# A decoder trunk of three token mixers: early weights in quarters, value products one accumulator at a time, an indexer that stays in PSUM, and last rows that end on three engines

## The chip, the cores and the metric

The kernel runs on one core of one Trainium2 chip. TensorE (PE) multiplies matrices, VectorE (DVE), ScalarE (ACT) and GpSimd (POOL) work on elements, and SyncE (SP) issues DMA transfers. The metric is the time of one execution in microseconds on the device.

## The reference

The input x has 512 rows of 1024 numbers. One projection feeds three mixers side by side: A, a pooling mixer with trailing windows of 2, 4, 8 and 16; B, sparse attention, in which an indexer scores the keys for each query and the 128 best are kept; C, attention in three branches (compressed blocks, selected blocks, a window), added with gates. Each is gated, projected to 1024 columns and merged; one output projection and a LayerNorm follow. What the change touches:

```python
rel = jax.nn.relu(jnp.einsum('bthd,bsd->bths', iqb, ik))          # B: the indexer
score = jnp.einsum('bths,bth->bts', rel, iwb).astype(jnp.float32)
...
_, idx = lax.top_k(score, topk)
...
p = _masked_softmax(s, valid).astype(v.dtype)
return jnp.einsum('bthk,btkd->bthd', p, vg)                       # B: the value product
...
p_c = _masked_softmax(s_c, m_c)                                   # C: compressed blocks
o_c = jnp.einsum('btgrn,bngd->btgrd', p_c.astype(vcmp.dtype), vcmp)
...
outs.append(mean - xg[:, :, g].astype(jnp.float32))               # A: window mean less x
...
return ((xf - mu) * lax.rsqrt(var + LN_EPS) * g + b).astype(x.dtype)
```

## The kernel before

**Products.** Every projection is computed in three matmuls for each piece of 128 inputs (L68 to L70): the operands are split into a high and a low part, and high x high, low x high and high x low are added in PSUM. The high part of a weight tile is made by ScalarE (L93 or L64), the low part by a subtraction on GpSimd (L95, in most of the program) or VectorE (L65). A tile of 128 output columns for all 512 rows takes 8 x 3 matmuls of 512 columns.

**Order.** TensorE executes in program order, and that order is written out by hand in `manual_schedule`. A stream of filler work F (projections, gates, merges) is stepped a few products at a time between the parts of the attention "units". The other engines' orders are chosen by the compiler's scheduler.

**Head.** Eight idle matmuls (L103) run while the first data arrives. The tiles of w0 and w3 come in halves, in turn with the eight pieces of x (L129), and the keys' projection takes two steps with w0, then two with w3.

**Indexer.** For row tiles 1 to 3 and eight heads a matmul writes 128 rows of scores in one of four PSUM slots ("qps"), ScalarE applies ReLU into a tile `rel` in SBUF (L292), and VectorE adds rel times a weight to `acc` (L294, L296). Sixteen rounds of MAX8 and MATCH_REPLACE (L305, L306) then find the best keys of each row tile.

**Attention units.** A unit is a row tile j of a branch: "c" units of branch C (g = 0, 1; two branches each), "b" units of branch B (b00 to b13: group, row tile). Its front computes query-key products in the same four slots (L442), mask and row extreme (L444), exponential (L449, ScalarE), the scale r (L453 to L457), and two f16 parts of the probabilities (pb or pc, L461 and L463), which a DMA transposes (L470). Its back, at least two sub-units later, is the value product (L480) into one of two halves of one PSUM bank (`ACC`), and `finish` (L535, VectorE) scales and gates it into yb or yc. `flush` takes units in pairs: both products stand next to each other in TensorE's order.

**Compressed blocks.** `Compressed.probs` subtracts the row extreme (L512, VectorE) and takes one exponential of four heads at once (L513). `compress_v` spreads the compressed values over a block-diagonal tile VC by multiplying with a 0/1 mask (L397, six VectorE instructions).

**End.** For each of four row tiles the output projection is followed by mean and variance and two passes, (z - mean) x gain (L925) and x scale + bias (L927). In tiles 0 to 2 VectorE does 768 columns and GpSimd 256; in the last tile VectorE does all 1024 in two pieces, each stored from SP's queue (L928).

Of the kernel before, what the change touches and what calls it, by code (L numbers as in the profile page):

```python
# [7 lines left out]
F32 = mybir.dt.float32  # L8
# [20 lines left out]
SMALL = (("posk", 32), ("posv", 32), ("pool_b", 4), ("pool_scale", 4), ("bmask", 4), ("rcnt", 16), ("rowv", 1),  # L29
# [5 lines left out]
def trunk(ctx, tc, a, out, dbg=None):  # L35
# [66 lines left out]
    for _ in range(8):  # L102
        nc.tensor.matmul(ps, idle[:, :128], idle, start=True, stop=True)  # L103
# [24 lines left out]
    with tc.high_priority():  # L128
        for k in "a01b23c4d567":  # L129
            if k in "abcd":  # L130
                load_early(EARLY["abcd".index(k) % 2], "abcd".index(k) // 2, 2)
            else:
                dma = load_x(int(k))
# [151 lines left out]
    def index_scores(j):  # L285
        n = (j + 1) * 128
        acc = cp.tile([128, n], F32, name=f"acc{j}")
        for h in range(8):
            ps = qps(f"is{j}{h}")[:, :n]
            nc.tensor.matmul(ps, QI[h][:, (j - 1) * 128:j * 128], KI[:, :n], start=True, stop=True)  # L290
            rel = big("b", "rel", F32, (128, 512))[:, :n]
            nc.scalar.activation(rel, ps, AF.Relu)  # L292
            if h == 0:
                nc.vector.tensor_scalar(acc, rel, IW[:, j, 0:1], None, op0=OP.mult)  # L294
            else:
                nc.vector.scalar_tensor_tensor(acc, rel, IW[:, j, h:h + 1], acc, op0=OP.mult, op1=OP.add)  # L296
            yield
        dg = acc[:, j * 128:n]
        nc.vector.tensor_add(dg, dg, cmask[:, 384:512])
        dbg(f"score{j}", acc)  # L300
        negm[j] = acc
# [13 lines left out]
    VC = [cp.tile([128, 2, 4, 64], BF, name=f"vc{p}") for p in range(3)]  # L315

# [65 lines left out]
    def compress_v():  # L382
        HH, HL, w2h, w2l = CP["v"] + W2[1]
        bmask = small["bmask"]
        v32 = sp.tile([128, 2, 64], F32, name="vc32", bufs=1)
        ps = dps("vc")[:, :128].rearrange("p (g d) -> p g d", g=2)
        for g in range(2):
            mm3(ps[:, g], HH[:, g].rearrange("p r n -> p (r n)"), HL[:, g].rearrange("p r n -> p (r n)"),
                w2h, w2l, True, True)
        nc.vector.tensor_scalar(v32, ps, vscale, 0.5, op0=OP.mult, op1=OP.mult)  # L390
        for p in range(3):
            v1 = sp.tile([128, 2, 64], BF, name="vc1", bufs=2)
            nc.vector.tensor_copy(v1, v32)
            if p < 2:
                nc.vector.tensor_sub(v32, v32, v1)
            for g in range(2):
                nc.vector.tensor_mul(VC[p][:, g], v1[:, g, None, :].to_broadcast([128, 4, 64]),  # L397
                                     bmask[:, :, None].to_broadcast([128, 4, 64]))
        yield
# [85 lines left out]
    class Compressed:  # L485
# [5 lines left out]
        def begin(self, j, Q, K):  # L491
# [4 lines left out]
            if j == NT - 1:  # L496
                ps = dps("sc")[:, :128].rearrange("p (h n) -> p h n", h=4)
                for h in range(4):
                    q = Q[h // 2][:, h % 2, j * 128:(j + 1) * 128]
                    for z in range(2):  # L500
                        nc.tensor.matmul(ps[:, h], q, K[:, z, :32], start=z == 0, stop=z == 1)
                nc.vector.tensor_add(self.s, ps, mcmp[:, j, None].to_broadcast([128, 4, 32]))
                nc.vector.tensor_reduce(self.mx[:, :4], self.s, AX.X, OP.max)

# [4 lines left out]
        def probs(self):  # L509
            g, j, s = self.g, self.j, self.s  # L510
            den, r = sm("cden", 4, 2), sm("cr", 4, 2)
            nc.vector.tensor_sub(s, s, self.mx[:, :4, None].to_broadcast([128, 4, 32]))  # L512
            nc.scalar.activation(s, s, AF.Exp, scale=self.scale)  # L513
# [43 lines left out]
    def pool_x(g):  # L557
# [14 lines left out]
        nc.vector.tensor_sub(e[:, :w - 1], e[:, :w - 1], x0[:, :w - 1])  # L572
        nc.vector.scalar_tensor_tensor(x0, cur, 1.0 / w, x0, op0=OP.mult, op1=OP.subtract)
        nc.vector.tensor_copy(x0[:, :w - 1], e[:, :w - 1])
# [157 lines left out]
    for n in (2, 1, 1, 1, 1, 1, 2):  # L732
# [48 lines left out]
    def flush(limit):  # L781

        while backs and (limit == 1000 or len(backs) > 1 and backs[1][0] <= limit):
            pair, n = backs[:2], 0
            del backs[:2]
            if limit == 1000:
                F.step(12)
            for _, un, (kind, g, j, br) in pair:
# [4 lines left out]
            for _, un, (kind, g, j, br) in pair:  # L793
# [13 lines left out]
    for w in work:  # L807
# [28 lines left out]
        backs.append((nsub, un, w))  # L836
# [63 lines left out]
    for t in range(NT):  # L900
# [15 lines left out]
        cut = (0, 512, 1024) if last else (0, 384, 768, 1024)  # L916
        cs = [slice(c0, c1) for c0, c1 in zip(cut, cut[1:])]
        if not last:
            c = cs.pop()
            nc.gpsimd.tensor_scalar(z[:, c], z[:, c], mv[:, 0:1], y, op0=OP.subtract, op1=OP.mult)  # L920
            nc.gpsimd.tensor_mul(z[:, c], z[:, c], lng[:, c])
            nc.gpsimd.tensor_add(z[:, c], z[:, c], lnb[:, c])
# [3 lines left out]
        for c in cs:  # L926
            nc.vector.scalar_tensor_tensor(z[:, c], z[:, c], y, lnb[:, c], op0=OP.mult, op1=OP.add)  # L927
            nc.sync.dma_start(out[t * 128:(t + 1) * 128, c], z[:, c])  # L928


def layout(v):
# [50 lines left out]
    r["bmask"] = (t[:, None] // 32 == np.arange(4)[None]).astype(f4)  # L982
# [19 lines left out]
```

## Time and profile before

| | |
|---|---|
| Median of 3 runs | 537.79 us (534.98 to 538.72) |
| The profiled execution | 536.65 us, of which the span of the profile is 534.9 |
| TensorE busy | 510.4 us (95%), 2718 matmuls |
| VectorE busy | 380.2 us (71%) |
| ScalarE busy | 278.4 us (52%) |
| GpSimd busy | 218.5 us (41%) |
| DMA | 66.72 MB, mean 125 GB/s |

The span is cut by stage as follows: until about 52 us the first projections, to about 92 the indexer beside other projections, to about 300 the units of branch C with the top-k rounds and the filler, to about 410 the units of branch B, then merges and the output projection, from 525.75 the last rows without TensorE. A matmul of 512 columns shows 0.39 us when TensorE has its full clock and 0.63 at the half; one starts 0.23 or 0.43 after the other. In a row of a timeline the bracket at the end is the idle time ahead of the instruction and what ended it.

### The profile page before, as it was taken

How to read it: one execution, taken by the hardware profiler on the slowest of the kernel's cores; microseconds unless marked ns; L12 is line 12 of the kernel's file. 1: busy time of each engine (PE TensorE's matmuls, PEld its weight loads, DVE VectorE, ACT ScalarE, POOL GpSimd, SP SyncE). 2: the span in 40 equal slices, each digit the busy share in tenths (PEclk: the TensorE clock that was granted, in tenths of full speed). 3: DMA queues.
4: the chain of work that ended last, by engine and by line, in shares of the span. 5: the costliest groups of instructions: out<-in, count | busy, mean ns of one | idle time of the engine just before them, and what ended most of it. 6: DMA issues, size and time to landing. Idle time of an engine off the chain costs nothing. (4 is left out here: it accounts for less than half of the span.)

```text
span 534.9 us, 7764 instructions
## 1 busy us (share of the span) xinstructions
PE 510.4 (95%) x2718; PEld 423.7 (79%) x2718; DVE 380.2 (71%) x928; ACT 278.4 (52%) x561; POOL 218.5 (41%) x190
## 2 busy tenths in 40 slices
PE   8999999999999998999998995999899999999993
PEld 5899878888888886788887884887787888887883
DVE  5774798898769898997898879565653345554276
ACT  6783465667655666565546564575553245342000
POOL 0425433436553756153534534227651212116043
PEclk9999989999999999999999998899999999999997
DMA  8622331363854434364545636256444435463012
GB/s 286 256 79 80 112 126 60 87 148 86 183 139 123 119 85 117 63 181 124 140 121 104 132 110 145 49 138 138 119 119 134 141 137 187 148 205 110 1 69 89
DMA packets 82135, 66.72 MB, mean 125 GB/s; under 512 B 67184, under 2 KB 68656, under 8 KB 82096
## 3 DMA queue, kind: packets, MB, share of 16 engines
q1 hardware_dynamic: 74912, 40.54, 28.5%
q0 software_dynamic: 7184, 25.69, 16.1%
q8 instruction: 21, 0.34, 0.3%
q14 instruction: 18, 0.15, 0.1%
HBM read 47.87 MB, written 2.10 MB: 93 GB/s over the span
## 5 line engine op out<-in xcount | busy, mean ns | idle before, releaser
L68 PE MATMUL d<-xh,w_h 128*128 128x512 f32 (+1 forms) x424 | 167.5, 395 | 2.6 <-ACT z L153 2.2
L69 PE MATMUL d<-xl,w_h 128*128 128x512 f32 (+1 forms) x424 | 165.8, 391 | 0.0
L70 PE MATMUL d<-xh,w_l 128*128 128x512 f32 (+1 forms) x424 | 165.5, 390 | 0.0
L95 POOL TENSOR_TENSOR w_l<-w_st,w_h 128x1024 fp32r<-128x1024 f32 x41 | 99.5, 2428 | 127.1 <-ACT w_h L93 120.4
L68 PEld LDWEIGHTS d<-xh,w_h 128*128 128x128 f32 x424 | 80.5, 190 | 18.3 <-ACT z L153 2.6
L70 PEld LDWEIGHTS d<-xh,w_l 128*128 128x128 f32 x424 | 80.3, 189 | 16.9
L69 PEld LDWEIGHTS d<-xl,w_h 128*128 128x128 f32 x424 | 80.4, 190 | 14.1
L93 ACT ACTIVATE w_h<-w_st 128x1024 fp32r<-128x1024 f32 x53 | 56.2, 1060 | 36.9 <-DMA w_st<-in_wt_dram 20.5
L449 ACT ACTIVATE qkc<-qkc,nb 128x512 f32<-128x512 f32 (+3 forms) x64 | 32.0, 501 | 49.8 <-DVE nb L444 32.0
L95 POOL TENSOR_TENSOR wp_l<-wp_st,wp_h 128x512 fp32r<-128x512 f32 x16 | 20.8, 1297 | 48.3 <-ACT wp_h L93 48.3
L641 POOL TENSOR_TENSOR m<-m,tg 128x512 f32<-128x512 f32 x12 | 17.5, 1457 | 54.2 <-DVE tg L615 54.0
L463 DVE SCALAR_TENSOR_TENSOR pc<-qkc,r,pc 128x512 f16<-128x512 f32 (+3 forms) x64 | 32.4, 544 | 8.2 <-ACT pc L461 7.9
L461 ACT ACTIVATE pc<-qkc,r 128x512 f16<-128x512 f32 (+3 forms) x64 | 29.5, 525 | 15.1 <-DVE r L457 7.2
L444 DVE CUSTOM_DVE_ANT_0 qkc<-qkc,cmask 128x512 f32<-128x512 f32 (+3 forms) x64 | 31.2, 493 | 2.9 <-PE qkc L442 2.5
L449 ACT ACTIVATE qkb<-qkb,nb 128x128 f32<-128x128 f32 (+3 forms) x32 | 16.0, 499 | 23.1 <-DVE nb L444 22.8
L92 POOL DMA_DIRECT2D w_st<-in_wt_dram x41 | 23.3, 569 | 9.9 <-POOL w_l L95 5.9
L70 PE MATMUL wo<-woh,ml 128*128 128x512 f32 (+1 forms) x72 | 26.4, 367 | 0.6 <-DVE ml L65 0.6
L69 PE MATMUL wo<-wol,mh 128*128 128x512 f32 (+1 forms) x72 | 26.3, 366 | 0.0
L68 PE MATMUL wo<-woh,mh 128*128 128x512 f32 (+1 forms) x72 | 26.3, 365 | 0.0
L306 DVE MATCH_REPLACE8 acc<-m,acc 128x256 f32<-128x256 f32 (+2 forms) x48 | 25.9, 541 | 0.0
L305 DVE MAX8 m<-acc 128x8 f32<-128x256 f32 (+2 forms) x48 | 25.2, 548 | 0.1
L68 PE MATMUL pp<-yh,wp_h 128*128 128x512 f32 x64 | 25.1, 392 | 0.0
(249 smaller groups left out, 1015.3 us busy)
## 6 DMA issues: line engine op xcount, KB each, us to landing
w_st<-in_wt_dram POOLq DMA_DIRECT2D x41, 512.0 KB, 3.7
w_st<-in_wt_dram SPq DMA_DIRECT2D x12, 512.0 KB, 4.4
wp_st<-in_wp_dram POOLq DMA_DIRECT2D x16, 256.0 KB, 3.0
wo_st<-in_wo_dram SPq DMA_DIRECT2D x8, 512.0 KB, 3.5
xst<-in_xT_dram SPq DMA_DIRECT2D x8, 256.0 KB, 4.8
wp_st<-in_wp_dram SPq DMA_DIRECT2D x8, 256.0 KB, 2.6
z<-in_x_dram SPq DMA_DIRECT2D x4, 512.0 KB, 5.1
wvst<-in_wve_dram SPq DMA_DIRECT2D x4, 320.0 KB, 7.1
```

The costliest lines, as they stand in the source:

```text
L68: nc.tensor.matmul(ps, wh, rh, start=start, stop=False)
L69: nc.tensor.matmul(ps, wh, rl, start=False, stop=False)
L70: nc.tensor.matmul(ps, wl, rh, start=False, stop=stop)
L92: (nc.gpsimd if POOL[0] else nc.sync).dma_start(st, src)
L93: nc.scalar.activation(h[:, :n], st, AF.Copy)
L95: eng.tensor_sub(l[:, :n], st, f(h[:, :n]))
L305: nc.vector.max(m8, negm[j])
L306: nc.vector.match_replace(negm[j], m8, negm[j], MARK)
L444: nc.vector.tensor_tensor_reduce(sc[i], sc[i], self.mask, -0.125, 3e38, OP.add, OP.min, nb[:, i:i + 1])
L449: nc.scalar.activation(sc[i], sc[i], AF.Exp, scale=-1.0, bias=nb[:, i:i + 1], accum_out=den[:, i:i + 1])
L461: nc.scalar.activation(p[:, 0, i], sc[i], AF.Copy, scale=r[:, i:i + 1])
L463: self.last = nc.vector.scalar_tensor_tensor(p[:, 1, i], sc[i], r[:, i:i + 1], p[:, 0, i], op0=OP.mult, op1=OP.subtract)
```

## The change

- The head has nine idle matmuls; w0 and w3 come in quarters, a quarter ahead of each piece of x, and the two streams of the keys' projection take turns step by step.
- The ReLU of the indexer writes back into the PSUM slot it reads; VectorE reads it there.
- VC is zeroed by GpSimd at the start and filled with twelve GpSimd copies of 32 partitions; the mask is gone.
- The compressed blocks' row extreme goes into the exponential as its bias, which takes four instructions of 32 columns on ScalarE for one; the VectorE subtraction is gone. For j = 3 a small VectorE scaling is added.
- In `pool_x` the edge columns are written in place, without the copy.
- `flush` takes a "b" unit as soon as its own turn has come; "c" units stay in pairs.
- The last row tile is cut 448, 448, 128: the last 128 columns are scaled on ScalarE (with an added column nm from VectorE), multiplied and added on GpSimd. Its three stores stand on SP's queue.

```diff
-    for _ in range(8):
+    for _ in range(9):
         nc.tensor.matmul(ps, idle[:, :128], idle, start=True, stop=True)
...
-        for k in "a01b23c4d567":
-            if k in "abcd":
-                load_early(EARLY["abcd".index(k) % 2], "abcd".index(k) // 2, 2)
-            else:
-                dma = load_x(int(k))
+        for k in range(KT):
+            load_early(EARLY[k % 2], k // 2, 4)
+            dma = load_x(k)
...
-            rel = big("b", "rel", F32, (128, 512))[:, :n]
+            rel = ps
             nc.scalar.activation(rel, ps, AF.Relu)
...
+    for p in range(3):
+        nc.gpsimd.memset(VC[p], 0.0)
...
-            for g in range(2):
-                nc.vector.tensor_mul(VC[p][:, g], v1[:, g, None, :].to_broadcast([128, 4, 64]),
-                                     bmask[:, :, None].to_broadcast([128, 4, 64]))
+            for h in range(4):
+                r = slice(32 * h, 32 * h + 32)
+                nc.gpsimd.tensor_copy(VC[p][r, :, h], v1[r])
...
+                nc.vector.tensor_scalar(self.mx[:, :4], self.mx[:, :4], -0.125, None, op0=OP.mult)
...
-            nc.vector.tensor_sub(s, s, self.mx[:, :4, None].to_broadcast([128, 4, 32]))
-            nc.scalar.activation(s, s, AF.Exp, scale=self.scale)
+            for h in range(4):
+                nc.scalar.activation(s[:, h], s[:, h], AF.Exp, scale=self.scale, bias=self.mx[:, h:h + 1])
...
-        nc.vector.tensor_sub(e[:, :w - 1], e[:, :w - 1], x0[:, :w - 1])
-        nc.vector.scalar_tensor_tensor(x0, cur, 1.0 / w, x0, op0=OP.mult, op1=OP.subtract)
-        nc.vector.tensor_copy(x0[:, :w - 1], e[:, :w - 1])
+        nc.vector.tensor_sub(x0[:, :w - 1], e[:, :w - 1], x0[:, :w - 1])
+        nc.vector.scalar_tensor_tensor(x0[:, w - 1:], cur[:, w - 1:], 1.0 / w, x0[:, w - 1:], op0=OP.mult,
+                                       op1=OP.subtract)
...
-    for n in (2, 1, 1, 1, 1, 1, 2):
+    for n in (1, 1, 1, 1, 1, 1, 1, 2):
...
-        while backs and (limit == 1000 or len(backs) > 1 and backs[1][0] <= limit):
-            pair, n = backs[:2], 0
-            del backs[:2]
+        while backs and (limit == 1000 or len(backs) >= backs[0][3] and backs[backs[0][3] - 1][0] <= limit):
+            pair, n = backs[:backs[0][3]], 0
+            del backs[:len(pair)]
             if limit == 1000:
-                F.step(12)
+                F.step(8)
...
-        backs.append((nsub, un, w))
+        backs.append((nsub, un, w, 2 if kind == "c" else 1))
...
-        cut = (0, 512, 1024) if last else (0, 384, 768, 1024)
+        cut = (0, 448, 896, 1024) if last else (0, 384, 768, 1024)
...
+        c = cs.pop()
+        if last:
+            m = sm("nm", 1)
+            nc.vector.scalar_tensor_tensor(m, mv[:, 0:1], -1.0, y, op0=OP.mult, op1=OP.mult)
+            nc.scalar.activation(z[:, c], z[:, c], AF.Identity, scale=y, bias=m)
+        else:
+            nc.gpsimd.tensor_scalar(z[:, c], z[:, c], mv[:, 0:1], y, op0=OP.subtract, op1=OP.mult)
+        nc.gpsimd.tensor_mul(z[:, c], z[:, c], lng[:, c])
+        nc.gpsimd.tensor_add(z[:, c], z[:, c], lnb[:, c])
...
+        if last:
+            nc.sync.dma_start(out[t * 128:(t + 1) * 128, 896:], z[:, 896:])
```

TensorE at the first two value products of branch B (`ptb_3437` and `ptb_3509` are the transposed probabilities of b00 and b01, both written into halves of `acc`), as it stands before:

```order
L480 LDWEIGHTS vl
L480 MATMUL acc_152<-ptb_3437,vl 64x256
L480 LDWEIGHTS vh
L480 MATMUL acc_152<-ptb_3437,vh 64x256
L480 LDWEIGHTS vh
L480 MATMUL acc_152<-ptb_3437,vh 64x256
L480 LDWEIGHTS vh
L480 MATMUL acc_152<-ptb_3509,vh 64x256
L480 LDWEIGHTS vh
L480 MATMUL acc_152<-ptb_3509,vh 64x256
```

The same place of the change, from the end of b00's product (`ptb_3449` here):

```order
L479 LDWEIGHTS vh
L479 MATMUL acc_168<-ptb_3449,vh 64x256
L441 MATMUL qkb_3647<-kb,bq_2545 128x384 x2
L68 MATMUL d_3612<-xh_86,w_h 128x512
L69 MATMUL d_3612<-xl_90,w_h 128x512
L70 MATMUL d_3612<-xh_86,w_l 128x512
L68 MATMUL d_3612<-xh_87,w_h 128x512
L69 MATMUL d_3612<-xl_91,w_h 128x512
L70 MATMUL d_3612<-xh_87,w_l 128x512
L68 MATMUL d_3612<-xh_87,w_h 128x512
L69 MATMUL d_3612<-xl_91,w_h 128x512
L70 MATMUL d_3612<-xh_87,w_l 128x512
```

b00's product now stands one sub-unit earlier, ahead of the query-key matmul of b02's second sub-unit; three more dense matmuls, the other query-key matmul and twelve dense ones follow before b01's product.

VectorE around yb of b00 before (`yb` is the finish, the ISA row the mask, `r` the scale of a sub-unit, `pb` a probability part):

```order
L453 RECIPROCAL r<-den 128x2
L306 MATCH_REPLACE acc_855<-m_3617,acc_855 128x512
L455 TENSOR_SCALAR r<-r 128x2
L463 SCALAR_TENSOR_TENSOR pb_3670<-qkb_3628,r,pb_3670 128x384
L463 SCALAR_TENSOR_TENSOR pb_3670<-qkb_3642,r,pb_3670 128x384
L305 MAX m_3676<-acc_855 128x8
L535 SCALAR_TENSOR_TENSOR yb_3378<-acc_152,yscale,zb_2642 128x2x128
L306 MATCH_REPLACE acc_855<-m_3676,acc_855 128x512
```

and in the change:

```order
L304 MATCH_REPLACE acc_855<-m_3526,acc_855 128x512
L452 RECIPROCAL r<-den 128x2
L454 TENSOR_SCALAR r<-r 128x2
L535 SCALAR_TENSOR_TENSOR yb_3390<-acc_168,yscale,zb_2648 128x2x128
L443 ISA qkb_3647,nb<-qkb_3647,acc_698 128x384
L443 ISA nb 128x1
L462 SCALAR_TENSOR_TENSOR pb_3619<-qkb_3580,r,pb_3619 128x384
L462 SCALAR_TENSOR_TENSOR pb_3619<-qkb_3594,r,pb_3619 128x384
```

yb of b00 has moved from behind the pb of b02's second sub-unit to ahead of that sub-unit's mask.

ScalarE in the units of branch C with g = 1, j = 3 (`cs` is the compressed blocks' scores, `z` in the last row the eviction of a projection), before:

```order
L513 ACTIVATE cs<-cs 128x128
L449 ACTIVATE qkc_2254,den<-qkc_2254,nb 128x512
L521 ACTIVATE cp<-cs 128x128
L461 ACTIVATE pc_2271<-qkc_2208,r 128x512
L461 ACTIVATE pc_2271<-qkc_2254,r 128x512
L93 ACTIVATE w_h<-w_st 128x1024
L406 ACTIVATE zc_1330<-d_2247,bhalf 128x512
L449 ACTIVATE qkc_2289,den<-qkc_2289,nb 128x512
L449 ACTIVATE qkc_2315,den<-qkc_2315,nb 128x512
L461 ACTIVATE pc_2332<-qkc_2289,r 128x512
L461 ACTIVATE pc_2332<-qkc_2315,r 128x512
L153 ACTIVATE z<-d_2247,bias 128x512
```

and in the change:

```order
L513 ACTIVATE cs<-cs,cmx 128x32 x4
L448 ACTIVATE qkc_2258,den<-qkc_2258,nb 128x512
L460 ACTIVATE pc_2275<-qkc_2213,r 128x512
L460 ACTIVATE pc_2275<-qkc_2258,r 128x512
L521 ACTIVATE cp<-cs 128x128
L93 ACTIVATE w_h<-w_st 128x1024
L405 ACTIVATE zc_1331<-d_2251,bhalf 128x512
L448 ACTIVATE qkc_2293,den<-qkc_2293,nb 128x512
L448 ACTIVATE qkc_2319,den<-qkc_2319,nb 128x512
L460 ACTIVATE pc_2336<-qkc_2293,r 128x512
L460 ACTIVATE pc_2336<-qkc_2319,r 128x512
L151 ACTIVATE z<-d_2251,bias 128x512
```

The four exponentials stand where the one stood; cp has moved behind the two pc; the rest up to the eviction z keeps its order.

## Rows read from the trace of the kernel before

**Rows 1.** The page, busy time: engine, us, share of the span, instructions.

```profile
PE 510.4 (95%) x2718; PEld 423.7 (79%) x2718; DVE 380.2 (71%) x928; ACT 278.4 (52%) x561; POOL 218.5 (41%) x190
```

**Rows 2.** Waits of TensorE: waiting tile and line, releaser: total us, times, longest.

```profile
PE acc L480 <- DVE yb L535: 8.0, 4, 5.5
PE d L68 <- ACT z L153: 2.2, 1, 2.2
...
PE pp L68 <- DVE m L615: 1.2, 1, 1.2
PE cpk L69 <- DVE bkl L65: 1.2, 1, 1.2
```

**Rows 3.** Windows: PE, PEld, DVE, ACT, POOL busy (instructions), granted clock, DMA share, GB/s.

```profile
52.00:100.00 48.00, 46.84 (x280) 39.47 (x279) 40.00 (x76) 27.55 (x52) 19.24 (x16) 0.96 0.26 83
200.00:250.00 50.00, 47.58 (x261) 38.59 (x260) 45.74 (x121) 30.08 (x60) 23.40 (x25) 0.97 0.52 124
326.00:340.00 14.00, 8.55 (x44) 6.49 (x43) 9.49 (x20) 4.28 (x9) 2.90 (x2) 0.76 0.41 107
```

**Rows 4.** Timeline of TensorE, 328 to 338 us: start, duration, instruction, [idle before].

```profile
328.22 0.28 PE L480 MATMUL acc<-ptb,vh 128*64 128x256 f16 x2
333.95 0.42 PE L480 MATMUL acc<-ptb,vh 128*64 128x256 f16 x2 [5.45 <-DVE yb L535]
...
336.39 0.63 PE L68 MATMUL d<-xh,w_h 128*128 128x512 f32 x1
...
337.64 0.39 PE L68 MATMUL d<-xh,w_h 128*128 128x512 f32 x1
337.87 0.40 PE L69 MATMUL d<-xl,w_h 128*128 128x512 f32 x1
```

**Rows 5.** Timeline of VectorE, 328 to 335 us.

```profile
329.01 2.06 DVE L455 TENSOR_SCALAR r<-r 128x2 f32<-128x2 f32 x1
...
333.43 0.47 DVE L535 SCALAR_TENSOR_TENSOR yb<-acc,yscale,zb 128x256 f32<-128x256 f32 x1
```

**Rows 6.** Single lines: min/median/max ns, first and last start, shapes.

```profile
L512 DVE TENSOR_TENSOR cs<-cs,cmx x8: 281/830/1653, 94.6 to 287.8; 128x128 f32<-128x128 f32 x8
...
L397 DVE TENSOR_TENSOR vc<-vc,small x6: 410/416/1240, 107.1 to 113.1; 128x256 bf16<-128x256 bf16 x6
...
L296 DVE SCALAR_TENSOR_TENSOR acc<-rel,iw,acc x21: 475/612/2465, 54.9 to 91.6; 128x256 f32<-128x256 f32 x7, 128x384 f32<-128x384 f32 x7, 128x512 f32<-128x512 f32 x7
...
L513 ACT ACTIVATE cs<-cs x8: 298/310/311, 97.5 to 288.2; 128x128 f32<-128x128 f32 x8
```

**Rows 7.** Timeline of ScalarE, 208 to 211 us.

```profile
209.04 1.26 ACT L461 ACTIVATE pc<-qkc,r 128x512 f16<-128x512 f32 x2 [0.83 <-ACT qkc L449]
210.20 0.69 ACT L153 ACTIVATE z<-d,bias 128x512 f32<-128x512 f32 x1
```

**Rows 8.** Timeline of all engines at 59.3 to 59.6 us.

```profile
59.33 2.39 POOL L95 TENSOR_TENSOR w_l<-w_st,w_h 128x1024 fp32r<-128x1024 f32 x1 [4.24 <-ACT w_h L93]
...
59.54 2.46 DVE L296 SCALAR_TENSOR_TENSOR acc<-rel,iw,acc 128x256 f32<-128x256 f32 x1
```

**Rows 9.** Timeline of all engines, from 527 us, the last rows.

```profile
527.26 0.72 POOL L922 TENSOR_TENSOR z<-z,lnb 128x256 f32<-128x256 f32 x1
...
527.36 1.83 DVE L925 SCALAR_TENSOR_TENSOR z<-z,mv,lng 128x512 f32<-128x512 f32 x2
...
529.75 1.41 DVE L927 SCALAR_TENSOR_TENSOR z<-z,rs,lnb 128x512 f32<-128x512 f32 x2
530.53 1.08 SPq L928 DMA_DIRECT2D out_dram<-z  x2
```

**Rows 10.** Timeline of TensorE, the first 10 us.

```profile
1.18 3.60 PE L103 MATMUL idle<-idle 128*128 128x512 bf16 x8 [1.18 <-DVE idle L100]
5.44 0.80 PE L68 MATMUL d<-xh,w0h 128*128 128x512 f32 x1 [0.67 <-ACT xh L64]
...
9.78 0.46 PE L68 MATMUL d<-xh,w3h 128*128 128x512 f32 x1
```

More of the change, by code (lines that the diff above doesn't have):

```diff
@@ L28 @@
 NTILES = I_G + 24
-SMALL = (("posk", 32), ("posv", 32), ("pool_b", 4), ("pool_scale", 4), ("bmask", 4), ("rcnt", 16), ("rowv", 1),
+SMALL = (("posk", 32), ("posv", 32), ("pool_b", 4), ("pool_scale", 4), ("rcnt", 16), ("rowv", 1),
          ("mcmp", 128), ("ident", 128))
@@ L383, in compress_v @@
         HH, HL, w2h, w2l = CP["v"] + W2[1]
-        bmask = small["bmask"]
         v32 = sp.tile([128, 2, 64], F32, name="vc32", bufs=1)
@@ L781, in flush @@
     def flush(limit):
-        while backs and (limit == 1000 or len(backs) > 1 and backs[1][0] <= limit):
-            pair, n = backs[:2], 0
-            del backs[:2]
+        while backs and (limit == 1000 or len(backs) >= backs[0][3] and backs[backs[0][3] - 1][0] <= limit):
+            pair, n = backs[:backs[0][3]], 0
+            del backs[:len(pair)]
             if limit == 1000:
-                F.step(12)
-            for _, un, (kind, g, j, br) in pair:
+                F.step(8)
+            for _, un, (kind, g, j, br), _ in pair:
                 if kind == "c":
@@ L792, in flush @@
                     F.until(("f_zb", g, 0), ("f_zb", g, 1))
-            for _, un, (kind, g, j, br) in pair:
+            for _, un, (kind, g, j, br), _ in pair:
                 for _ in un.back(br == 0):
@@ L915, in trunk @@
         nc.vector.scalar_tensor_tensor(y, e, 3.0, y, op0=OP.subtract, op1=OP.mult)
-        cut = (0, 512, 1024) if last else (0, 384, 768, 1024)
+        cut = (0, 448, 896, 1024) if last else (0, 384, 768, 1024)
         cs = [slice(c0, c1) for c0, c1 in zip(cut, cut[1:])]
+        c = cs.pop()
[7 more added lines that the diff above has]
+        nc.gpsimd.tensor_add(z[:, c], z[:, c], lnb[:, c])
         if not last:
[L919 to L922, printed above, removed]
             nc.sync.dma_start(out[t * 128:(t + 1) * 128, c], z[:, c])
@@ L981, in layout @@
     r["rowv"] = (t >= 31).astype(f4)[:, None]
-    r["bmask"] = (t[:, None] // 32 == np.arange(4)[None]).astype(f4)
     r["rcnt"] = c(np.broadcast_to((1.0 / np.arange(1, 17)).astype(f4), (128, 16)))
```

## The prediction, made before the change was run

> **What bounds the kernel now.** I read the page first. TensorE is busy for 510.4 of 534.9 us [rows 1] and the change gives it one matmul more and none less, so the time can only come from the 24.5 us in which it is idle and from the stretches in which it runs at the lower of its two clocks. Then the list of what TensorE waits for [rows 2]: one line holds 8.0 us, the value products of the sparse branch (L480) waiting for VectorE's yb (L535), 5.5 of it in one go; the next three, for ScalarE's z and for VectorE's m and bkl, come to 2.2 + 1.2 + 1.2 = 4.6. Then the windows by stage [rows 3]: VectorE is at 45.74 of 50 us between 200 and 250, so it is nearly a second bound there, and the granted clock is 0.96, 0.97 and 0.76 in the three stretches that hold waits and 1.00 elsewhere. Last the timelines around the waits and of both ends.
>
> The long wait reads so [rows 4, 5]. The product of unit b00 is issued until 328.22 + 0.28 = 328.5. The next product, of b01, stands right behind it, writes the other half of the same PSUM bank, and starts at 333.95, 0.05 us after yb (333.43 + 0.47) has read the first. VectorE wasn't free: a two-element scaling took 2.06 us from 329.01 and the queue in front of yb is in order. After it TensorE runs matmuls of 0.63 us (1.2 GHz) until 337.64, where they take 0.39 again (2.4 GHz): 3.7 us at half speed, about 1.7 lost.
>
> **The change part by part.** The sum stands against the profiled run's own 536.65 us (span 534.9 and 1.75 around it), which is 1.1 under the median of 537.79.
>
> *Sparse branch, one product per accumulator.* The order puts a query-key matmul and 12 to 15 dense ones between b00's product and b01's. At 0.23 us each (337.64 to 337.87 [rows 4]) that is about 3 us in which yb can run, and on VectorE yb now stands ahead of the next mask, not behind the next unit's scalings. All four waits (8.0) and the slow stretch (1.7) are at stake: between 0 and -9.7. What is late next is the end of the last top-k, which the following unit's mask needs; but VectorE is idle for 14 - 9.49 = 4.5 us of that stretch [rows 3], so it can catch up, and the query-key tiles have four buffers. The product moves one sub-unit nearer to its transposing DMA; the compressed and window units' second products already stand at that distance, and no wait for a transposed tile is in [rows 2]. I take -9.0, since two of the four waits are near 0.6 and may stay in part.
>
> *Less VectorE work.* Gone are eight subtractions of 0.83 us in the middle (6.6 us), six multiplications of VC (five of 0.416 and one of 1.24, 3.3 us), four short copies in pool_x, and what the indexer's accumulations take over their undisturbed time [rows 6]. Added are two small scalings. That is some 10 us of VectorE or a little more between 52 and 336, but VectorE isn't on TensorE's path for most of it. The 4.6 us of waits there and the two slow stretches (0.04 x 48 = 1.9 and 0.03 x 50 = 1.5) give the ends: 0 and -8.0. Row by row little of it must go: in the 2.2 us wait, z on ScalarE (210.20) stands behind the two pc (209.04) that wait for VectorE [rows 7], and ScalarE's order keeps it there; the wait for bkl lies behind bias additions that the change leaves. I take -1.5.
>
> One accumulation takes 2.46 us, with the w_l subtraction on GpSimd (59.33, 2.39) beside it [rows 8]; the quickest of the same line takes 0.475 [rows 6]. With rel left in PSUM the instruction has one operand in SBUF. The Trainium skill, "SBUF — State Buffer", section "Who interferes with whom", says that a VectorE instruction with two SBUF inputs and a GpSimd one that reads SBUF shut each other out, and one with a single SBUF input doesn't take part. The rows agree; by it the collisions of the indexer go, which is in the term above.
>
> *What goes to other engines.* ScalarE gets 32 exponentials for 8. One of 128 elements takes 0.31 [rows 6], so four small ones are at most 1.24, +0.9 per unit, with ScalarE at 30.08 of 50 us [rows 3]; hidden by that idle time, and the price without cover is the rival below. GpSimd gets 12 copies of 32 partitions and three memsets: each between nothing and the 2.39 of a w_l [rows 8], and I take 0.36, half of the 0.72 of the nearest row, an addition of twice the columns [rows 9]: 12 x 0.36 = 4.3 us. They stand ahead of two weight subtractions and two weight transfers in GpSimd's queue, for which GpSimd's own idle time there is the cover: none of the waits in [rows 2] is for a w_l. So 0, and +3 at most if a weight comes that much too late.
>
> *Indexer.* A PSUM slot is held until VectorE has read it rather than until ScalarE's ReLU. The 21 accumulations begin over 91.6 - 54.9 = 36.7 us [rows 6], so a step comes every 1.8 us and four slots give 7.3 us from a matmul to the end of its accumulation. Between 0 and one more wait like the 1.2 of bkl; I take 0.
>
> *Head.* Eight idle matmuls fill 1.18 to 4.78, then 0.67 us pass until xh is there, and the first nine real ones (5.44 to 9.78) run at 0.48 each instead of 0.23, 2.2 us lost [rows 10]. An idle one takes 3.60 / 8 = 0.45, so the ninth fills the gap to 5.23; with a quarter of w0 in front of x instead of a half, xh can only land earlier. Start -0.2; the second matmul waits for xl, which follows xh, so up to -0.5 in all. If the clock rises as much earlier as the gap was long, or at once, up to -1.8 more. I take -1.2 for the head, between 0 and -2.3. The Trainium skill, "TensorE: Matmul & The Clock Gate", Part 1, says the clock's watch runs free of the program, so that the moment of the rise differs from run to run. By that page the head is worth only its -0.5 on average and the sum 0.7 more. No row of one run can show it.
>
> *Tail.* The two passes over the last rows take 1.83 and 1.41 us for two pieces of 512 [rows 9]; 448 columns are one eighth less, -0.2 on each pass at most, -0.3 in all. The added nm is one more step of one column; between the end of the first pass (527.36 + 1.83) and the start of the second (529.75) three such steps take 0.56, so 0.2. A third store in SP's queue costs 1.08 / 2 = 0.54 behind the second. ScalarE and GpSimd finish 128 columns beside VectorE, in less than its 1.3 us. The first pass took 1.83 against 1.41 for the second while GpSimd's addition (0.72) ran beside it; the same may now befall the second pass, +0.4. So +0.5, between -0.3 and +1.2. By the section of the Trainium skill named above ("SBUF — State Buffer") that collision must come, as both engines read two SBUF operands; the sum would then be 0.4 longer.
>
> Sum: 536.65 - 9.0 - 1.5 - 1.2 + 0.5 = 525.45. The runs' median lies 1.1 above the profiled run, so about **526**; own range of this case 521 to 530.
>
> **The rivals.**
> 1. *The wait only moves.* VectorE is still late at 329 to 334, so b01's product goes at once, but a mask or a query-key tile is late a few us on. For it: ahead of yb VectorE's queue held 333.43 - 329.01 = 4.4 us of other work [rows 5]. Against: the 4.5 us of its idle time right behind, which came from TensorE's own lateness. Half of the sparse branch's term stays: 536.65 - 4.9 - 0 - 0.5 + 0.5 = 531.8, with the median's offset 532 to 533. Chance 0.16.
> 2. *All stalls go.* VectorE's 11 us bring every wait in the middle to nothing, with both slow stretches, and the head's clock rises at once: 536.65 - 9.7 - 8.0 - 2.3 + 0 = 516.7; with one of the waits left 518. Against it is ScalarE's unchanged order around z. Chance 0.13.
> 3. *ScalarE becomes late: slower.* The four exponentials stand in ScalarE's queue between others' exponentials and the projections' evictions. Each of the eight compressed units would then hold TensorE by 0.9 and, as after 210.94, send it into a slow stretch of 1.5: 8 x 2.4 = 19 us, 525.5 + 19 = 545. It decides once ScalarE's idle time ahead of an eviction that TensorE waits for is under 0.9 us; ahead of the pc at 209.04 it is 0.83 [rows 7], so there it is near, but over 200 to 250 a full 20 us are idle. Chance 0.06.
> 4. *No effect.* The products now wait for their transposed tiles or the next yb as long as before, and the copies on GpSimd delay weights by 3: 534 to 538. Chance 0.07.
>
> **How the numbers follow.** The likeliest case has 0.58 and gives 526. The range leaves out half of rival 2, and rivals 3 and 4: 518.5 to 533.5. One per cent, 5.4 us, is what I take a measurement of this kernel to tell from none: faster means under 532.4. That is the main case, rival 2 and half of rival 1, 0.58 + 0.13 + 0.08 = 0.79; within it the other half and rival 4, 0.15; slower 0.06.
>
> **What would show it.** In the profile after: L480 gone from TensorE's waits or under 1 us in all, and no slow matmuls near 330 (right), or the same microseconds under L442 or L480 with another releaser (rival 1). The wait for z near 210 should still be there at 1 to 2 us; its absence speaks for rival 2. The first real matmul at about 5.2 with the pitch at 0.23 before 9. The indexer's accumulations all near 0.5 to 0.7. From the first pass over the last rows (527.36) to the span's end 7.5 us before, about 8 then. Waits with ScalarE as releaser, ahead of L68, would prove me wrong toward rival 3; waits for w_l, on GpSimd's copies.

## The result, and the profile after

The changed kernel takes 531.56 us (median of 7 runs, 531.19 to 533.42) against 537.79 (7 runs): ratio 0.990, 95% interval 0.987 to 0.993. That is 6.2 us faster, at the edge of the one per cent; 526 was forecast. The profiled execution takes 531.56 with a span of 529.8, so 5.1 us less than the one of before.

What TensorE waits for in the changed kernel (waiting tile, releaser: total us, times, longest), to be laid beside [rows 2]:

```profile
PE qkc L441 <- DVE pc L462: 3.3, 3, 1.6
PE d L68 <- ACT z L151: 2.4, 1, 2.4
...
PE wo L70 <- DVE ml L65: 1.1, 1, 1.1
PE pp L68 <- DVE m L615: 0.9, 1, 0.9
PE cpk L69 <- DVE bkl L65: 0.6, 1, 0.6
```

The 8.0 us of the value products are gone altogether. At the head of the list stands a line that [rows 2] do not have: query-key products of branch C's units that wait for VectorE's pc, the last reader of their PSUM slot. The windows that answer to [rows 3]:

```profile
52.00:100.00 48.00, 47.13 (x285) 38.91 (x284) 39.89 (x76) 28.32 (x55) 18.93 (x16) 1.00 0.27 86
200.00:250.00 50.00, 46.95 (x264) 38.01 (x263) 45.26 (x122) 31.59 (x69) 24.59 (x26) 1.00 0.49 125
326.00:340.00 14.00, 14.00 (x71) 11.26 (x70) 12.97 (x29) 8.72 (x17) 6.88 (x6) 1.00 0.52 133
```

TensorE is busy for all 14 us from 326 to 340 (8.55 before), at the full clock. The timeline of TensorE there, which answers to [rows 4]:

```profile
329.44 0.30 PE L479 MATMUL acc<-ptb,vh 128*64 128x256 f16 x2
...
330.22 0.73 PE L441 MATMUL qkb<-kb,bq 128*128 128x512 f32 x2
...
333.53 0.62 PE L441 MATMUL qkb<-kb,bq 128*128 128x512 f32 x2
```

b01's product starts without a bracket, and the dense work follows without one. VectorE (answers to [rows 5]) has had yb ready for 2.6 us:

```profile
326.01 0.44 DVE L454 TENSOR_SCALAR r<-r 128x2 f32<-128x2 f32 x1
326.36 0.47 DVE L535 SCALAR_TENSOR_TENSOR yb<-acc,yscale,zb 128x256 f32<-128x256 f32 x1
```

TensorE's last matmul ends at 518.46 instead of 526.03 (525.75 + 0.28 of the last row of its timeline), 7.6 us earlier; the span is only 5.1 shorter. The end, then, has become 2.5 us longer: 11.3 us from the last matmul, 8.8 before. GpSimd and the store queue there:

```profile
519.70 0.72 POOL L926 TENSOR_TENSOR z<-z,lnb 128x256 f32<-128x256 f32 x1
522.88 0.84 POOL L925 TENSOR_TENSOR z<-z,lng 128x128 f32<-128x128 f32 x1 [2.46 <-ACT z L922]
523.80 0.45 POOL L926 TENSOR_TENSOR z<-z,lnb 128x128 f32<-128x128 f32 x1
```

```profile
522.84 0.93 SPq L933 DMA_DIRECT2D out_dram<-z  x2
524.28 0.33 SPq L935 DMA_DIRECT2D out_dram<-z  x1
```

The third store is issued at 524.28 and lands 1.6 us later, at 525.9; the span goes on to 529.8. What lies between is read from the last line of the program, whose instructions on GpSimd's queue are a drain, first of the changed kernel and then of before (shortest, median and longest ns, first and last start):

```profile
L1004 POOLq DRAIN  x3: 40/102/5236, 523.8 to 529.5; - x3
```

```profile
L998 POOLq DRAIN  x3: 40/93/5504, 527.2 to 534.6; - x3
```

The long one is the first. It begins when GpSimd's last instruction does and ends at 523.8 + 5.2 = 529.0 here, and at 527.2 + 5.5 = 532.7 before. In both that is 4.75 us after GpSimd's last instruction has ended (524.25; 527.26 + 0.72 = 527.98 in [rows 9]), and the same holds in the traces of all eleven experiments below. Before, the last store, issued at 531.3, landed 2.4 us later, at 533.7, and covered it. In the changed kernel nothing does.

### The profile page after: what moved, and what is told of

Read it like the earlier page. It is cut to its first block, busy times and chain, and to the rows that moved or that the text cites. A ratio compares the mean times of both kernels' runs of the same rounds, so it can differ in the third digit from the quotient of the medians.

```text
span 529.8 us, 7808 instructions
## 1 busy us (share of the span) xinstructions
PE 506.9 (96%) x2719; PEld 418.0 (79%) x2719; DVE 377.6 (71%) x917; ACT 282.3 (53%) x590; POOL 222.4 (42%) x207
## 4 chain that ended last, share of the span: by engine, by line
PE 51%; DVE 4%; DMA 2%; ACT 1%; issue 1%; POOL 0%; POOLq 0%; ACTq 0%
PE d L68 9%; PE d L69 9%; PE d L70 9%; PE pp L68 4%; PE pp L69 4%; PE pp L70 4%; PE acc L479 3%; PE wo L70 3%; PE wo L68 2%; PE wo L69 2%; PE qkb L441 2%; DMA wo_st<-in_wo_dram 2%; PE qkc L441 1%; DVE wol L65 1%; DVE pc L462 1%
## 5 line engine op out<-in xcount | busy, mean ns | idle before, releaser
L95 DVE TENSOR_TENSOR w_l<-w_st,w_h 128x1024 fp32r<-128x1024 f32 x12 | 15.9, 1327 | 13.8 <-ACT w_h L93 13.8
L65 DVE TENSOR_TENSOR wol<-wo_st,woh 128x1024 fp32r<-128x1024 f32 x8 | 10.7, 1339 | 20.6 <-ACT woh L64 17.2
```

Source lines behind the costliest of these rows:

```text
L95: eng.tensor_sub(l[:, :n], st, f(h[:, :n]))
```

## The experiments

Two things had to be explained: 2.5 us at the end, and new waits of 3.3 us for pc. Theory A: the end waits for GpSimd's closing drain, and the change gave GpSimd work in the last row tile. Its rival was the third store. Theory B: the four exponentials of a compressed unit shifted ScalarE's order. Its rival was VC's move to GpSimd, and later ScalarE's added time. Each run was timed beside the kernel before on the same chip, in three sets: e1 to e4, e5 to e8, e9 to e11. Between sets the ratios are what can be compared.

**e1: the end put back.**

```diff
 # the changed kernel, but:
-        cut = (0, 448, 896, 1024) if last else (0, 384, 768, 1024)
+        cut = (0, 512, 1024) if last else (0, 384, 768, 1024)
...
         if not last:
+            c = cs.pop()
             nc.gpsimd.tensor_scalar(z[:, c], z[:, c], mv[:, 0:1], y, op0=OP.subtract, op1=OP.mult)
```

> The changed kernel with the end of the kernel before: last row tile cut 512, 512 on VectorE, two stores, no ScalarE or GpSimd piece; the order of every engine ahead of the end is the same. Theory A (the end of the program waits for GpSimd's closing drain, which lasted 4.75 us after its last instruction in both traces: 527.98 to 532.73 before, 524.25 to 529.00 after): GpSimd's last instruction is now the addition of row tile 2, over 3.5 us earlier, so the drain is under the stores again and the span from the last matmul falls from 11.3 to about 8.8 us: 531.6 - 2.5 = 529.1 us. Rival (the third store of 64 KB is the cost, its issue and landing): 1.6 to 2 us of landing stay with any last store, so only its 0.5 us of issue go: 531.0.

528.35 us, ratio to before 0.984 (0.981 to 0.987): 3.2 less than the changed kernel. The last matmul stays where it was (518.59), the span ends 8.1 us behind it instead of 11.3. The drain is over at 519.8 + 5.5 = 525.3 and the span ends at 526.6:

```profile
L997 POOLq DRAIN  x3: 40/93/5504, 519.8 to 526.4; - x3
```

**e2: a GpSimd instruction at the end of the kernel before.**

```diff
             nc.sync.dma_start(out[t * 128:(t + 1) * 128, c], z[:, c])
+    nc.gpsimd.tensor_copy(sm("tl", 1), z[:, 1023:1024])
```

> The kernel before with one GpSimd copy of one column, read from the last rows after VectorE's last pass, into a tile nobody reads. Theory A (closing drain of GpSimd): its last instruction ends at about 531.5 instead of 528.0, the drain 4.75 us later at 536.2, the span's end 0.7 behind that, 537.0 instead of 534.9: +2.0 us, about 539.8 median. Rival (third store): no store is added, so no change beyond noise, 537.8.

539.46 us, ratio 1.003 (1.001 to 1.006): +1.7 us for a copy of one column that nobody reads. The copy and its drain, from the two views used above:

```profile
533.51 0.19 POOL L929 COPY tl<-z 128x1 f32<-128x1 f32 x1 [3.24 <-DVE z L927]
```

```profile
L999 POOLq DRAIN  x3: 40/93/4954, 533.5 to 539.0; - x3
```

533.5 + 4.95 = 538.45, again 4.75 us after the instruction's end at 533.70; the span ends 0.8 us later. From the last matmul (528.32) to the end it is 10.9 us, against 8.8.

**e11: three stores, but nothing on GpSimd.** The changed kernel with the last 128 columns on VectorE.

```diff
         c = cs.pop()
-        if last:
-            m = sm("nm", 1)
...
+        if not last:
+            nc.gpsimd.tensor_scalar(z[:, c], z[:, c], mv[:, 0:1], y, op0=OP.subtract, op1=OP.mult)
...
+        else:
+            cs.append(c)
```

> The changed kernel, last row tile still cut 448, 448, 128 with three stores on one queue, but the last 128 columns on VectorE too; nothing of the last tile on ScalarE or GpSimd. Theory A (GpSimd's closing drain): GpSimd is done at 520.5, VectorE needs 0.4 to 0.5 more, the third store is issued about when it was in the changed kernel (524.3) and lands 1.6 to 2 later, so the end is at about 527 instead of 529.8: 528.7. Rival (the third store): as the changed kernel or slower, 531.6 to 532.

529.56 us, ratio 0.983 (0.979 to 0.987), 2.0 less than the changed kernel. The end is 8.7 us long with three stores: 2.6 less than in the changed kernel, and 0.6 more than the 8.1 of e1, which has two. So the third store costs about 0.6 us where the stores end last; in the changed kernel the drain covers it. Theory A holds in all three runs.

**e3: the compressed blocks' probabilities put back.**

```diff
-            for h in range(4):
-                nc.scalar.activation(s[:, h], s[:, h], AF.Exp, scale=self.scale, bias=self.mx[:, h:h + 1])
+            nc.vector.tensor_sub(s, s, self.mx[:, :4, None].to_broadcast([128, 4, 32]))
+            nc.scalar.activation(s, s, AF.Exp, scale=self.scale)
```

> The changed kernel with the compressed blocks' probabilities as before: VectorE subtraction and one exponential of 128 columns instead of four of 32 with the extreme as bias. Theory B (the four exponentials shift ScalarE's order: a weight conversion and an eviction now stand between the two pc of a sub-unit, which hold the query-key PSUM slots, and TensorE waits for them, 1.5 + 0.2 + 1.6 = 3.3 us at 113, 121 and 129): ScalarE's order has the two pc together again, those three waits go, 531.6 - 3.3 = about 528.5. Rival (VC's copies on GpSimd and the casts that VectorE now makes for them cause the lateness at 103 to 113): the waits stay, and VectorE gets 6.6 us more: 531.6 to 533.

527.81 us, ratio 0.983 (0.980 to 0.986): 3.75 us less than the changed kernel. No wait for pc is left, and the last matmul ends at 514.60 instead of 518.46. ScalarE around the first of the three waits, in the changed kernel:

```profile
110.75 1.05 ACT L93 ACTIVATE w_h<-w_st 128x1024 fp32r<-128x1024 f32 x1
111.69 0.68 ACT L460 ACTIVATE pc<-qkc,r 128x512 f16<-128x512 f32 x1
112.26 0.68 ACT L603 ACTIVATE eg<-d,bhalf 128x512 f32<-128x512 f32 x1
112.83 0.69 ACT L460 ACTIVATE pc<-qkc,r 128x512 f16<-128x512 f32 x1
```

and in e3:

```profile
107.90 1.26 ACT L460 ACTIVATE pc<-qkc,r 128x512 f16<-128x512 f32 x2 [3.12 <-DVE r L456]
109.05 0.66 ACT L448 ACTIVATE qkc<-qkc,nb 128x512 f32<-128x512 f32 x1
...
109.71 1.06 ACT L93 ACTIVATE w_h<-w_st 128x1024 fp32r<-128x1024 f32 x1
110.66 0.69 ACT L602 ACTIVATE eg<-d,bhalf 128x512 f32<-128x512 f32 x1
```

In e3 both pc run before the weight conversion w_h; in the changed kernel w_h stands ahead of the first and an eviction (eg) between the two. VectorE's pc follows ScalarE's and is the last to read the query-key slot, so TensorE's next product waits 1.53 us.

The third wait, of 1.57 us, comes about differently. There the two pc stand together, and ScalarE has been idle for 2.34 us before them: they wait for the scale r. All engines in the changed kernel:

```profile
122.05 0.14 DVE L452 RECIPROCAL r<-den 128x2 f32<-128x2 f32 x1
...
124.16 2.72 POOL L95 TENSOR_TENSOR w_l<-w_st,w_h 128x1024 fp32r<-128x1024 f32 x1
...
124.94 1.95 DVE L456 TENSOR_TENSOR r<-r,gs 128x2 f32<-128x2 f32 x1
...
126.98 1.26 ACT L460 ACTIVATE pc<-qkc,r 128x512 f16<-128x512 f32 x2 [2.34 <-issue]
...
128.83 0.65 PE L441 MATMUL qkc<-ks,cq 128*128 128x416 f32 x2 [1.57 <-DVE pc L462]
```

The second step of r (L456) begins 2.9 us behind its first (L452), with other work between them in VectorE's order, and takes 1.95 us beside GpSimd's w_l; its median is 0.16. In the seven traces with the old probabilities (before, e2, e3, e5 to e8) the second step begins at most 0.33 us behind the first at all three places; in those with the four exponentials, e9 aside, 0.9 to 2.9. So the edit moved r back in VectorE's order as well as pc in ScalarE's.

**e4: VC put back on VectorE.** The mask, the six multiplications and the constant return; the GpSimd memsets and copies go.

```diff
-            for h in range(4):
-                r = slice(32 * h, 32 * h + 32)
-                nc.gpsimd.tensor_copy(VC[p][r, :, h], v1[r])
+            for g in range(2):
+                nc.vector.tensor_mul(VC[p][:, g], v1[:, g, None, :].to_broadcast([128, 4, 64]),
+                                     bmask[:, :, None].to_broadcast([128, 4, 64]))
```

> The changed kernel with VC filled as before, by six VectorE multiplications with the mask, no GpSimd copies. Theory B (four exponentials): ScalarE's order keeps the weight conversion between the two pc, so the waits of TensorE for pc at 113 to 129 stay at 3 us or grow by VectorE's 3.3 us: 531.6 to 533. Rival (VC's copies): the waits at 113 and 121 go, 529.5 to 530.

531.18 us, ratio 0.990 (0.986 to 0.994), the same as the changed kernel. The waits for pc come to 2.9 us, but they are not the same ones: 2.7 at 113.65 and 0.2 at 127.49. At the first of them the two pc stand together (112.13), and w_h and the eviction ran long before them (106.26, 107.23). ScalarE then sits idle for 3.55 us, because VectorE is late: r's second step comes 2.9 us behind its first (108.36, 111.28), with VC's work among what lies between. So VC's move is worth nothing that can be measured, and the waits do not go with it; and lateness on VectorE makes TensorE wait even where ScalarE's order holds nothing up.

**e9: the four exponentials kept, pc given priority.** The end is put back too, so the partner is e1.

```diff
-                for i in range(b * hb, b * hb + hb):
-                    nc.scalar.activation(p[:, 0, i], sc[i], AF.Copy, scale=r[:, i:i + 1])
+                with tc.high_priority():
+                    for i in range(b * hb, b * hb + hb):
+                        nc.scalar.activation(p[:, 0, i], sc[i], AF.Copy, scale=r[:, i:i + 1])
```

> The changed kernel with the end put back (528.35 us), its 32 small exponentials kept, and the ScalarE pc of every sub-unit given priority in the scheduler, so that in ScalarE's order the two pc at 111 to 113, and later ones, stand next to each other ahead of the weight conversion. Theory B1 (the order is the cost): with the two conversions out of the way the first wait for pc shrinks from 1.5 to about 0.6 and the other two go, 3.3 to under 1.2 us, 526 to 526.5. Rival B2 (ScalarE's longer work, four exponentials and their fixed time, or VectorE's r behind the second mask, is the cost): waits of 3 us stay, 528 to 528.5.

524.78 us, ratio 0.976 (0.973 to 0.979): 3.6 us less than e1 in the medians, more than was expected of it; in the traces the last matmul comes 2.6 us earlier (516.01 against 518.59). The one line of its list on pc, which replaces the 3.3 us:

```profile
PE qkc L441 <- DVE pc L463: 0.9, 1, 0.9
```

All 32 small exponentials are still there, so most of the cost is not ScalarE's time but the order. Two orders have changed, though. At the first wait the eviction no longer stands between the two pc; w_h is still ahead of both, and 0.9 us are left. At the third, which gives 1.8 of the 2.6 us, the pc stood together before; what moved is r on VectorE, whose second step now follows the first at once and takes 0.16 us, clear of w_l:

```profile
119.94 0.15 DVE L452 RECIPROCAL r<-den 128x2 f32<-128x2 f32 x1
...
120.13 0.16 DVE L456 TENSOR_TENSOR r<-r,gs 128x2 f32<-128x2 f32 x1
```

How much of that is r's place in the order and how much the meeting with w_l, no run separates. Against e5 below, which has the old probabilities, 0.8 us are left in the medians.

**e10: the probabilities alone, on the kernel before.** The two hunks of `Compressed` as in the change and nothing else.

```diff
+                nc.vector.tensor_scalar(self.mx[:, :4], self.mx[:, :4], -0.125, None, op0=OP.mult)
...
-            nc.vector.tensor_sub(s, s, self.mx[:, :4, None].to_broadcast([128, 4, 32]))
-            nc.scalar.activation(s, s, AF.Exp, scale=self.scale)
+            for h in range(4):
+                nc.scalar.activation(s[:, h], s[:, h], AF.Exp, scale=self.scale, bias=self.mx[:, h:h + 1])
```

> The kernel before with only the compressed blocks' probabilities changed: four exponentials of 32 columns for one, no VectorE subtraction. In ScalarE's order of this kernel the two pc of each of the first sub-units stand together. Theory B1 (order): no waits for pc, and VectorE's 6.6 us give 0 to 1: 537 to 538. Rival B2 (the exponentials' own time): TensorE waits about 3 us for pc, 541.

539.36 us, ratio 1.002 (1.000 to 1.004), 1.7 more than its partner: neither number was met. There is no wait for pc, as B1 says, but this does not decide for B1. The two pc stand together, yet w_h (110.39) and the eviction (111.34) are ahead of both (111.91), and VectorE's first pc is done at 113.38, later than the 113.15 of the changed kernel. TensorE does not wait because it comes there only at 113.53; in the changed kernel it was there at 111.68. The loss is of the size by which the long wait for yb has grown, from 5.5 to 7.1 us.

**e5: both put back, the rest of the change kept.** The edits of e1 and e3 together.

```diff
-        cut = (0, 448, 896, 1024) if last else (0, 384, 768, 1024)
+        cut = (0, 512, 1024) if last else (0, 384, 768, 1024)
...
+            nc.vector.tensor_sub(s, s, self.mx[:, :4, None].to_broadcast([128, 4, 32]))
+            nc.scalar.activation(s, s, AF.Exp, scale=self.scale)
```

> The changed kernel with both the end and the compressed blocks' probabilities of the kernel before. If the two costs found (GpSimd's closing drain, 2.5 to 3.2 us; the split pc on ScalarE, 3.7 us) are separate, they add: TensorE's last matmul at about 514.6 as with the probabilities alone, 8.1 us of end behind it, 531.6 - 2.5 - 3.8 = 525.3, between 524.3 and 526. Rival (both runs gained by a chance of the schedule or of the head): less than the better one alone improves, 527 to 528.

523.97 us, ratio 0.975 (0.972 to 0.977). The two costs add: 531.56 - 3.2 - 3.75 = 524.6. This is the fastest version of the study, 7.6 us under the changed kernel.

**e6: the sparse branch's products alone, on the kernel before.** The `flush` and `backs.append` hunks of the change and nothing else.

```diff
-        backs.append((nsub, un, w))
+        backs.append((nsub, un, w, 2 if kind == "c" else 1))
```

> The kernel before with only the product of each sparse unit issued by itself. Prediction's term: -9.0 of at most -9.7 (8.0 of waits, 1.7 of slow clock): 537.8 - 9 = 528.8. Rival 1 of the prediction (VectorE stays late and the wait moves): -4.9, 533.

527.98 us, ratio 0.983 (0.981 to 0.986). The last matmul moves from 526.03 to 516.68, 9.35 us. All four waits are gone and no other has grown; its list of waits begins with the three that [rows 2] show behind them:

```profile
PE d L68 <- ACT z L153: 2.2, 1, 2.2
...
PE pp L68 <- DVE m L615: 1.2, 1, 1.2
PE cpk L69 <- DVE bkl L65: 1.1, 1, 1.1
```

**e8: the indexer in PSUM, VC and pool_x alone, on the kernel before.**

```diff
-            rel = big("b", "rel", F32, (128, 512))[:, :n]
+            rel = ps
```

> The kernel before with the indexer in PSUM, VC's copies on GpSimd and pool_x without its copy, and nothing else. Prediction's term for less VectorE work: -1.5, between 0 and -8: 536.3. If ScalarE's unchanged order holds z (2.2 us near 210) and the bias additions hold bkl (1.2 near 72), nothing moves but the slow stretches: 536 to 538; if VectorE's lateness was the cause of all, 530.

535.52 us, ratio 0.994 (0.992 to 0.996), 2.7 less than its partner; in the trace the last matmul is 1.1 us earlier. The wait for z stays (2.1), that for bkl falls from 1.2 to 0.4.

**e7: halves instead of quarters, in e5.** The loads and the steps of the keys' streams as before, nine idle matmuls.

```diff
-        for k in range(KT):
-            load_early(EARLY[k % 2], k // 2, 4)
-            dma = load_x(k)
+        for k in "a01b23c4d567":
...
-    for n in (1, 1, 1, 1, 1, 1, 1, 2):
+    for n in (2, 1, 1, 1, 1, 1, 2):
```

> As the run with end and probabilities put back, and also w0 and w3 in halves in the order of the kernel before; nine idle matmuls stay. Theory C (quarters move 128 KB in 1 KB pieces per partition, the DMA engines are full from 5 us on and carry 312 and 330 GB/s instead of 353 and 390, so x, w0, w3 and the first weights land 1.5 to 2.2 us later and the clock's gain of 1.9 us is lost again by 29 us): with halves the first real matmul starts at 5.3, the gap is closed by the ninth idle one, the gain stays, and it is 1 to 1.6 us faster than the run with quarters: about 524. Rival (the early pace is bound by w3's first half, which is whole only at 8.4): no gain or a slower start, 525.3 to 526.

524.98 us, ratio 0.977 (0.975 to 0.980); e5 has 523.97, with intervals that overlap. The first projections end 0.9 us earlier than in e5 (36.57 against 37.45), but the last matmul only 0.45 (513.84 against 514.29), and the last store landed later. Inconclusive for the time; the loss of the quarters by 37 us is in the trace, as theory C has it. At 71 us e7 is 1.2 ahead; it loses 1.6 between 210 and 213, in slow matmuls behind the wait for z, which the trace of e5 does not have.

## Why the prediction was wrong

The forecast was 526, the kernel takes 531.6. That this lies beside rival 1's sum of 531.8 is chance: the wait of rival 1 is not there. Term by term:

- **Sparse branch, -9.0: right.** e6 measures 9.35 in the trace and 1.7% in time; rival 1, that the wait only moves, is refuted. The cover was reckoned too small, and that was luck: not 3 us but 7.0 lie between the end of b00's product (322.44) and the start of b01's (329.44), with 27 dense and two query-key products. yb is done 4.4 us after b00's product, so 3 us would have left a wait of 1.4.
- **Less VectorE work, -1.5: right in size.** e8: 1.1 in the trace, 2.7 in the medians. The wait for z stayed, in every run, for the reason given: ScalarE's order around it. TensorE's slow stretch at 52 to 100 is gone: the granted clock there is 1.00 in all nine traces with the indexer in PSUM, 0.93 to 0.96 in the four without. That at 200 to 250 is absent after, but not by the edit: behind the same wait for z the clock is 1.00 in the changed kernel, e3, e4 and e5 and 0.97 in e1, e7, e8, e9 and e11. The accumulation of 2.46 us is gone as well; the longest of that line is now 0.75, as in all nine of those traces, against 2.46 in the four others:

```profile
L294 DVE SCALAR_TENSOR_TENSOR acc<-is,iw,acc x21: 474/611/754, 54.0 to 89.9; 128x256 f32<-128x256 f32 x7, 128x384 f32<-128x384 f32 x7, 128x512 f32<-128x512 f32 x7
```

  The median, 611 ns, is what it was (612): what went is one collision, not a cost of each instruction. That agrees with the section "Who interferes with whom" of "SBUF — State Buffer" in the Trainium skill, which the prediction drew on.
- **What goes to other engines, 0: failed.** This is the first step that broke: "hidden by that idle time". The price per unit was, if anything, too high. Four of 0.31 stand for one of 0.31, and where they stand in a row one starts 0.21 after the other, so they add about 0.64, not 0.9:

```profile
L513 ACT ACTIVATE cs<-cs,cmx x32: 307/310/339, 93.5 to 289.2; 128x32 f32<-128x32 f32 x32
```

  Idle time of 20 us in 50 does not say who stands ahead of whom. ScalarE's order was set beside that of before at one place, g = 1 and j = 3, where only cp had moved; that says nothing of the first units of branch C. There pc had moved behind w_h and an eviction on ScalarE, and r behind other work on VectorE, and TensorE lost 3.9 us by the last matmul (518.46 against 514.60 in e3): about 1.5 at the first wait for pc, 0.5 at the second, 1.8 at the third. Rival 3 named ScalarE, but priced its time; e9 shows that the order is most of the cost, and the traces that it is the order of two engines.
- **Tail, +0.5: failed.** The rows of the end were priced to the last store, and behind it the same end as before was assumed. GpSimd's drain, which in the trace of before is over 1.0 us ahead of the last store's landing, has no term. Measured: +2.5 in the profile against before, 3.2 in the medians against e1. nm cost 0.16 as estimated, and the third store 0.6 in e11, near the 0.54 of the sum, but here it lies under the drain. The collision that was expected in the second pass fell on GpSimd: its product took 0.84 us, its addition of the same size 0.45, while VectorE's two pieces took 0.68 each, as in e11 with GpSimd idle. The drain begins from GpSimd's last instruction, so this too went into the end.
- **Head, -1.2: half right.** The clock came early: real matmuls at 0.23 from the third on, 1.9 us ahead after 12 of them (8.66 against 10.54). By 38 us only 0.33 is left. The DMA windows show why, the change first, then before (last columns: DMA share, GB/s):

```profile
5.00:10.00 5.00, 4.46 (x17) 3.11 (x18) 3.18 (x7) 2.93 (x7) 0.00 (x0) 1.00 0.98 312
10.00:15.00 5.00, 4.78 (x21) 3.60 (x21) 3.98 (x8) 3.85 (x9) 0.00 (x0) 1.00 1.01 330
```

```profile
5.00:10.00 5.00, 4.56 (x10) 3.16 (x11) 3.61 (x7) 3.77 (x7) 0.00 (x0) 1.00 0.98 353
10.00:15.00 5.00, 5.00 (x23) 4.09 (x23) 3.66 (x6) 3.94 (x6) 0.00 (x0) 1.00 1.04 390
```

  The engines are full in both, and with quarters they carry 12 and 15% less; with halves again and nine idle matmuls (e7) it is 367 and 404. The last piece of x lands at 14.5 instead of 12.3, the first full weight tile behind it at 15.9 instead of 13.9. On the clock the prediction set the Trainium skill's "TensorE: Matmul & The Clock Gate", Part 1, against its own sum. The runs agree with the page in part: of five traces with eight idle matmuls one (e10) had reached the full clock by the third real one, the others by the seventh to tenth; of eight with nine all but one (e9) had by the fourth. The moment varies, as the page says, but with the ninth it came earlier, in e7 with its halves too.

Put together in the trace: -9.35 - 1.1 + 3.9 + 2.5 - 0.3 = -4.4 of the -5.1 measured; the 0.7 that is left was not traced to one edit. The missing slow stretch behind the wait for z can hold it: e1, which has that stretch, loses 1.2 us there against the changed kernel. With the two failed terms as forecast, 0 and +0.5, it would have been 531.56 - 3.9 - 2.0 = 525.7, and e5, which takes both back, has 523.97.

## What to carry to other kernels

Look at what the last instruction of every engine is followed by: an engine that is idle at the end can be given work there only as far as its own closing time allows. And when an edit adds instructions to an in-order queue, compare the order, on that engine and on the others that the scheduler orders anew, at each place where a buffer is freed for the bottleneck, not the share of idle time: the same four instructions cost 3.7 us in one order (the changed kernel against e3) and 0.8 in another (e9 against e5).

## What the runs showed of the hardware

- GpSimd's closing drain ends 4.75 us after its last instruction, whichever that is, in all thirteen traces: 527.98 to 532.73 before, 524.25 to 529.00 after, 533.70 to 538.45 in e2.
- An exponential of 32 columns takes ScalarE as long as one of 128: 0.310 us in the median for both. Small ones in a row start 0.21 us after one another.
- A VectorE product of two columns (r, L456) took 2.13 and 1.95 us beside a GpSimd subtraction of 2.4 and 2.7 us in the changed kernel; its median there is 0.16.
- A GpSimd copy of 32 partitions and 128 columns took 0.287 us in the median.
